# The first layer's late modulation on TensorE or on VectorE, in a two-layer hybrid trunk

## The chip, the cores and the metric

The kernel runs on one core of a Trainium2 chip. The metric is the device time of one execution, in microseconds (us), as the median of several. The engines are TensorE (PE, its weight loads PEld), VectorE (DVE), ScalarE (ACT), GpSimd (POOL) and SyncE (SP), which issues most transfers.

## The reference, cut to what matters

Two streams of tokens (1024 latent, 128 context) go through two layers and a last norm. Each layer takes six vectors per stream from a modulation: a product of one conditioning vector per stream (c and c_ctx) with a 1024 x 6144 weight.

```python
for l in range(DEPTH):                                  # 2 layers
    mod_ctx = silu(c_ctx)[None, :] @ w_mod[l] + b_mod[l]
    mod_lat = silu(c) @ w_mod[l] + b_mod[l]
    ...
def trunk_layer(x, mod, p, ...):
    sh1, sc1, g1, sh2, sc2, g2 = split(mod, 6)
    u = rmsnorm(x, norm1_g) * (1 + sc1) + sh1
    x = x + g1 * token_mixers(u)     # GLA | RG-LRU | Hyena | HGRN2
    u = rmsnorm(x, norm2_g) * (1 + sc2) + sh2
    x = x + g2 * ((silu(u @ w1) * (u @ w3)) @ w2)
```

The Hyena mixer needs filters that depend on weights alone: small networks, a decay, a normalisation and a cosine/sine transform, for both layers and for both sequence lengths ("s" for 1024 tokens, "p" for 128).

## The kernel before, in words

The whole kernel is one program without loops on the chip. Activations lie transposed, 128 channels by 1152 tokens, in large SBUF tiles of the pool `dp` (tag "d", 19 buffers of 128 x 2312 floats). Weights come in through SP into `wr` and are split into two parts by ACT and DVE (`wsplit`, L339 and L340); projections are three matmuls per 128 x 384 block.

The order of the work is made in two steps. Python generators say in which order it is written: a `main` generator is advanced turn by turn, and after each turn the queue `s.queue` of projections ("fill") is advanced by so many nanoseconds of TensorE work (`weave`, `WB = 1800`). The tile framework then lays out each engine's instruction stream ahead of the run; it may put an instruction or a transfer ahead of its written place when its operands and a free buffer are planned to be there, and each engine then runs its stream in order. SP's transfers are such a stream too.

The modulation comes in 12 chunks of 512 columns per layer (`c`), each in two loads (`i`) of 1024 KB into a "d" tile `wm` (L417). There are two ways to compute a chunk:

- `mods_pe` (L436): for each of 4 x 128 rows of a load and each of four 128-column pieces, one matmul with the conditioning columns `cT` (32 columns, two of them in use) as the stationary operand. The four pieces go to four groups of 32 partitions of one PSUM tile `ps` of tag "a". After each load there is a yield.
- `mods_dve` (L455): for each of 4 x 128 rows of a load and each of the two streams, one VectorE instruction multiplies 512 columns by a per-partition scalar and adds them to the accumulator `macc` (L466 for the first, L468 for the rest). There is a yield after each two, so four per load. After the second load eight small matmuls with `es` sum `macc` over the partitions.

Both end in `mod_out` (L423): ACT copies the PSUM tile to `mp`, one matmul with `sel8` puts it in place, DVE adds the bias; two yields.

Chunks 0 to 3 of the first layer (`NM[0] = 4`) are computed on TensorE at the start, beside the first filters and the loading of x; the first norm needs them. Chunks 4 to 11 come in `late()` in `main` (L1926), which takes turns with the remaining filters: `t1, s1` (taps and spectra of the second layer's "s" filter, 11 and 17 turns) and `tp0, sp0, tp1, sp1` (the "p" filters, 7 turns each), 56 turns in all. When `late` ends it queues `v_proj(0, 1, ...)`, a projection (9 blocks of 24 matmuls, 128 x 272). After the weave the first HGRN2 projections ("h0") are queued, and `layer` begins with the two RG-LRU units (`rg_core`: weight tile `rgw` at L1580, DVE convolutions L1002 and L1005 on `rgx`, matmuls, ACT and DVE chains on `rgri` and `rgab`). The second layer's modulation is computed with `mods_dve` in the first layer's feed-forward (`side`).

```python
def late():
    macc = s.d("macc")[:, :1024].rearrange("p (x n) -> p x n", x=2)
    yield from s.mods_dve(0, na, 12, macc, 1)
    s.fill_add([s.v_proj(0, 1, st.u, st.vh)], ("vh", 0))
s.weave(s.turns([ch(t1, s1, tp0, sp0, tp1, sp1), late()]), s.WB)
```

Of the kernel before, what the change touches and what calls it, by code (L numbers as in the profile page):

```python
# [277 lines left out]
class Trunk:  # L278
# [1550 lines left out]
    def main(s):  # L1829
# [5 lines left out]
        with tc.tile_pool(name="dp", bufs=19) as dp, tc.tile_pool(name="gp", bufs=1) as gp, \  # L1835
# [62 lines left out]
            for w, o in (("s", 0), ("p", 1152)):  # L1898
                n = HC[w]["Q"]
# [13 lines left out]
            na, nb = s.NM  # L1913
            for _ in s.turns([ch(t0, itertools.islice(s0, nb)), xi, s.mods_pe(0, 0, na, s.AH)]):
                pass
            x, xt, y = box
# [7 lines left out]
            s.x_out(0, xt)  # L1924

            def late():  # L1926
                macc = s.d("macc")[:, :1024].rearrange("p (x n) -> p x n", x=2)
                yield from s.mods_dve(0, na, 12, macc, 1)
                s.fill_add([s.v_proj(0, 1, st.u, st.vh)], ("vh", 0))
            s.weave(s.turns([ch(t1, s1, tp0, sp0, tp1, sp1), late()]), s.WB)  # L1930
            s.fill_add(s.hgrn_items(0, st.u, 0, st.hb[0]), ("h0", 0))
            for l in range(DEPTH):
# [15 lines left out]
```

## Time and profile before

| | |
|---|---|
| median of 3 runs | 3421.86 us (3419.73 to 3423.37) |
| profiled execution | 3423.5 us |
| its span, first to last instruction | 3421.7 us |
| PE busy | 3301.0 us (96%) |
| DVE busy | 1848.7 us (54%) |
| ACT busy | 1017.9 us (30%) |
| mean granted TensorE clock | 0.978 |

The granted clock is given as a share of 2.4 GHz: 1.00 is that level, 0.50 is 1.2 GHz, and a value between is a stretch that holds both. A busy time multiplied by it is the work as it would last at 2.4 GHz. Times in the trace count from the start of the span. A matmul of 32-bit floats appears as two records.

### The profile page before, as it was taken

Reading aid. Unit: us, or ns where it says so; the run is one execution under the profiler, and the core shown is the slowest. Engines: PE = TensorE matmul, PEld = TensorE weight load, DVE = VectorE, ACT = ScalarE, POOL = GpSimd, SP = SyncE. Lnnn points to the kernel's source line nnn. Section 1 sums busy time; section 2 is a strip of 40 time slices with the busy share of each in tenths; the row PEclk is TensorE's granted clock in tenths of the full one; section 3 lists DMA queues with packets and bytes.
Section 4 is the critical chain, followed back from the end, with each engine's and each line's share of the span. In section 5 each row is a group of like instructions: output and inputs, shape, how many; then the busy total and the mean of one; then the engine's idle time right before and its main releaser. Section 6 shows DMA issues by size and latency. Waiting matters only on the chain. (4 is left out here: it accounts for less than half of the span.)

```text
span 3421.7 us, 55255 instructions
## 1 busy us (share of the span) xinstructions
PE 3301.0 (96%) x23502; PEld 3036.4 (89%) x23502; DVE 1848.7 (54%) x3872; ACT 1017.9 (30%) x1831; POOL 28.4 (1%) x101
## 2 busy tenths in 40 slices
PE   7977999999999999999999999999999999999998
PEld 3525888889999999999999887889999999999998
DVE  6866677666664443444448578564845222222326
ACT  4424445332232111111124635533323111111122
POOL 0000000000000000000000000000000000000000
PEclk8977999999999999999999999999999999999999
DMA  7251110113312121222122010112411111111112
GB/s 273 96 181 59 33 38 22 47 58 139 115 56 84 58 87 56 87 74 84 56 84 85 29 56 16 33 64 100 154 37 45 36 48 38 43 41 47 44 44 74
DMA packets 72995, 241.10 MB, mean 70 GB/s; under 512 B 14319, under 2 KB 26469, under 8 KB 60972
## 3 DMA queue, kind: packets, MB, share of 16 engines
q1 hardware_dynamic: 70844, 223.22, 19.0%
q0 software_dynamic: 1904, 14.35, 1.2%
q8 instruction: 185, 3.03, 0.4%
q14 instruction: 62, 0.51, 0.0%
HBM read 207.99 MB, written 29.56 MB: 69 GB/s over the span
## 5 line engine op out<-in xcount | busy, mean ns | idle before, releaser
L296 PE MATMUL pm<-u,ws 128*128 128x384 f32 x9792 | 1807.8, 341 | 14.8 <-DVE DS L851 6.1
L296 PEld LDWEIGHTS pm<-u,ws 128*128 128x128 f32 x9792 | 1706.4, 188 | 47.9 <-issue 9.4
L296 PE MATMUL ps<-hid,ws 128*128 128x384 f32 x3168 | 557.5, 337 | 0.0
L296 PEld LDWEIGHTS ps<-hid,ws 128*128 128x128 f32 x3168 | 552.1, 188 | 0.6 <-DVE hid L1750 0.2
L339 ACT CAST ws<-wr 128x1024 fp32r<-128x1024 f32 (+3 forms) x234 | 220.3, 941 | 666.5 <-PE ps L296 401.9
L340 DVE TENSOR_TENSOR ws<-wr,ws 128x1024 fp32r<-128x1024 f32 (+3 forms) x234 | 254.5, 1088 | 221.3 <-ACT ws L339 220.3
L1748 DVE TENSOR_TENSOR sg<-sg,pm 128x384 f32<-128x384 f32 x132 | 72.9, 553 | 467.6 <-PE pm L296 467.6
L1492 DVE SCALAR_TENSOR_TENSOR x<-ps,mod,x 128x256 f32<-128x256 f32 (+1 forms) x320 | 158.1, 515 | 275.6 <-PE ps L296 274.5
L1749 ACT CAST hid<-sg 128x384 fp32r<-128x384 f32 x132 | 67.8, 513 | 476.3 <-DVE sg L1748 476.1
L296 PE MATMUL pm<-mh,ws 128*128 128x384 f32 x1152 | 204.1, 338 | 0.7 <-DVE x L1492 0.7
L296 PEld LDWEIGHTS pm<-mh,ws 128*128 128x128 f32 x1152 | 201.3, 188 | 1.6 <-DVE x L1492 1.4
L1742 ACT ACTIVATE sg<-pm 128x384 f32<-128x384 f32 x132 | 64.5, 489 | 226.7 <-PE pm L296 226.7
L296 PE MATMUL pm<-ws,u 128*128 128x272 f32 (+1 forms) x864 | 117.1, 292 | 3.7 <-ACT ws L339 2.2
L296 PEld LDWEIGHTS pm<-ws,u 128*128 128x128 f32 x864 | 109.7, 191 | 7.9 <-ACT ws L339 2.5
L468 DVE SCALAR_TENSOR_TENSOR acc<-wm,cT,acc 128x512 f32<-128x512 f32 x168 | 116.0, 744 | 0.0
L680 DVE COPY_PREDICATED DS<-masks,ps 128x192 f32<-128x192 uint8 x288 | 92.4, 367 | 33.9 <-PE ps L296 33.9
L1750 DVE TENSOR_TENSOR hid<-sg,hid 128x384 fp32r<-128x384 f32 x132 | 73.5, 557 | 58.4 <-ACT hid L1749 58.4
L296 PEld LDWEIGHTS ps<-QQ,kc 64*64 64x64 f32 x3456 | 68.5, 134 | 40.1 <-issue 27.8
L677 DVE TENSOR_TENSOR KK<-KK,TT 128x384 f32<-128x384 f32 x168 | 99.9, 597 | 7.1 <-PE ps L296 5.3
L681 DVE TENSOR_TENSOR QQ<-QQ,TT 128x384 f32<-128x384 f32 x168 | 100.1, 596 | 0.1
L296 PE MATMUL ps<-QQ,kc 64*64 64x64 f32 x3456 | 88.3, 231 | 7.7 <-DVE kc L658 4.7
L539 ACT ACTIVATE sq<-x 128x384 f32<-128x384 f32 x84 | 43.7, 523 | 142.1 <-DVE x L1492 109.0
(312 smaller groups left out, 2777.3 us busy)
## 6 DMA issues: line engine op xcount, KB each, us to landing
wm<-w_mod SPq DMA_DIRECT2D x48, 1024.0 KB, 6.3
wr<-w SPq DMA_DIRECT2D x96, 512.0 KB, 3.2
wr<-w_in SPq DMA_DIRECT2D x48, 512.0 KB, 3.6
dft<-dft_s POOLq DMA_DIRECT2D x12, 1152.0 KB, 7.5
wr<-w SPq DMA_DIRECT2D x32, 320.0 KB, 3.0
xscr<-x SPq DMA_DIRECT2D x8, 1152.0 KB, 10.7
x<-xscr SPq DMA_DIRECT2D x8, 1152.0 KB, 5.2
wr<-w_out SPq DMA_DIRECT2D x16, 512.0 KB, 3.8
```

Source lines behind the costliest of these rows:

```text
L296: return s.nc.tensor.matmul(out, lhsT, rhs, start=start, stop=stop)
L339: nc.scalar.copy(w[:, 0, :n], raw[:, :n])
L340: nc.vector.tensor_tensor(out=w[:, 1, :n], in0=raw[:, :n], in1=w[:, 0, :n].bitcast(F32), op=ALU.subtract)
L468: nc.vector.scalar_tensor_tensor(out=acc[:, x], in0=wk, scalar=cc, in1=acc[:, x], op0=ALU.mult, op1=ALU.add)
L677: nc.vector.tensor_tensor(out=ka, in0=ka, in1=cap(TT, o + GS + h, [[2 * h, n], [-(GS + h), 2], [0, h]]), op=ALU.mult)
L680: nc.vector.copy_predicated(Dt[:, g, j], s.masks[:, li].unsqueeze(1).to_broadcast([128, 3, 64]), ps[j])
L681: nc.vector.tensor_tensor(out=qa, in0=qa, in1=cap(TT, o + h, [[2 * h, n], [GS - h, 2], [0, h]]), op=ALU.mult)
L1492: nc.vector.scalar_tensor_tensor(out=x[k][:, a:b], in0=ps[:, a - g * GS:b - g * GS], scalar=gcol[:, k, st:st + 1], in1=x[k][:, a:b], op0=A ...
L1742: nc.scalar.activation(out=sg, in_=ps, func=AF.Silu)
L1748: nc.vector.tensor_tensor(out=sg, in0=sg, in1=pp[1], op=ALU.mult)
L1749: nc.scalar.copy(hi[:, 0, sl], sg)
L1750: nc.vector.tensor_tensor(out=hi[:, 1, sl], in0=sg, in1=hi[:, 0, sl].bitcast(F32), op=ALU.subtract)
```

## The change

`late()` computes chunks 4 to 11 of the first layer with `mods_pe` in place of `mods_dve`, with two loads ahead in place of one. The accumulator `macc` goes. The loads, their number and size, `mod_out` and the second layer's modulation stay as they are. `late()` has 4 yields for each chunk (two loads, two in `mod_out`) in place of 10, so 32 in place of 80.

```diff
             def late():
-                macc = s.d("macc")[:, :1024].rearrange("p (x n) -> p x n", x=2)
-                yield from s.mods_dve(0, na, 12, macc, 1)
+                yield from s.mods_pe(0, na, 12, 2)
                 s.fill_add([s.v_proj(0, 1, st.u, st.vh)], ("vh", 0))
```

The function that is called now:

```python
def mods_pe(s, l, c0, c1, ahead):
    todo = [(c, i) for c in range(c0, c1) for i in range(2)]
    q = collections.deque(s.mod_load(l, c, i) for c, i in todo[:ahead])
    for at, (c, i) in enumerate(todo):
        w = q.popleft()
        if i == 0:
            ps = s.p("a")[:, :128]
        for k in range(4):
            for j in range(4):
                s.mm(ps[32 * j:32 * j + 32], s.cT[:, 2 * (4 * i + k):2 * (4 * i + k) + 32],
                     w[:, 512 * k + 128 * j:512 * k + 128 * j + 128], start=(i == 0 and k == 0), stop=(i == 1 and k == 3))
        if at + ahead < len(todo):
            q.append(s.mod_load(l, *todo[at + ahead]))
        yield
        if i == 1:
            yield from s.mod_out(l, c, ps)
```

## Rows read from the trace of the kernel before

**Rows 1.** The page: busy us, share and count; PE's busy tenths in 40 slices.
```profile
PE 3301.0 (96%) x23502; PEld 3036.4 (89%) x23502; DVE 1848.7 (54%) x3872; ACT 1017.9 (30%) x1831; POOL 28.4 (1%) x101
PE   7977999999999999999999999999999999999998
```

**Rows 2.** Windows: stretch, length, PE PEld DVE ACT POOL busy (count), PEclk, DMA share, GB/s.
```profile
118.00:158.00 40.00, 36.26 (x180) 27.08 (x179) 33.67 (x58) 15.63 (x31) 0.00 (x0) 0.93 0.29 98
158.00:203.00 45.00, 42.58 (x123) 17.17 (x123) 30.97 (x48) 11.69 (x22) 0.00 (x0) 0.95 0.54 176
203.00:300.00 97.00, 57.61 (x185) 19.32 (x183) 80.21 (x137) 24.05 (x42) 0.00 (x0) 0.58 0.36 123
300.00:383.00 83.00, 77.06 (x440) 71.00 (x441) 41.55 (x53) 57.34 (x78) 0.00 (x0) 0.96 0.09 26
383.00:900.00 517.00, 504.52 (x5332) 449.06 (x5331) 357.25 (x882) 197.76 (x394) 12.74 (x40) 1.00 0.21 71
```

**Rows 3.** Windows of the tile macc alone: PE, PEld, DVE busy us (count).
```profile
118.00:158.00 40.00, 0.65 (x16) 0.38 (x16) 14.38 (x22) 0.93 0.29 98
158.00:203.00 45.00, 1.50 (x32) 0.69 (x32) 17.64 (x28) 0.95 0.54 176
203.00:300.00 97.00, 5.34 (x80) 2.31 (x80) 52.33 (x79) 0.58 0.36 123
```

**Rows 4.** Waits from 203 to 300 us: us in total, times, longest.
```profile
PE ps L296 <- DVE fX L1138: 12.8, 2, 7.1
PE ps L296 <- DVE fH L1181: 8.8, 2, 4.9
...
PE ps L296 <- DMA rgw<-rg_w: 5.8, 1, 5.8
```

**Rows 5.** Timeline of DVE inside the third filter's taps: start, us, instruction.
```profile
205.92 0.74 DVE L1131 SCALAR_TENSOR_TENSOR fH<-ps,fw,fwn 48x512 f32<-48x512 f32 x1
206.59 1.40 DVE L468 SCALAR_TENSOR_TENSOR macc<-wm,cT,macc 128x512 f32<-128x512 f32 x2
...
208.51 0.74 DVE L1131 SCALAR_TENSOR_TENSOR fH<-ps,fw,fwn 48x512 f32<-48x512 f32 x1
```

**Rows 6.** Tile wm: ns min/median/max, first and last start.
```profile
L468 DVE SCALAR_TENSOR_TENSOR macc<-wm,cT,macc x112: 621/744/754, 124.3 to 297.7; 128x512 f32<-128x512 f32 x112
L466 DVE TENSOR_SCALAR macc<-wm,cT x16: 466/481/487, 123.5 to 288.7; 128x512 f32<-128x512 f32 x16
```

**Rows 7.** Timeline of PE: start, us, matmuls and their count.
```profile
31.58 3.64 PE L296 MATMUL pa<-wm,cT 128*32 128x128 f32 x64
...
148.34 0.65 PE L296 MATMUL pa<-macc,es 128*32 128x128 f32 x16
...
255.60 1.08 PE L296 MATMUL pa<-macc,es 128*32 128x128 f32 x16
...
314.28 12.55 PE L296 MATMUL pm<-ws,u 128*128 128x272 f32 x96
...
330.35 10.12 PE L296 MATMUL pm<-u,ws 128*128 128x384 f32 x57
```

**Rows 8.** Timeline of SP's queue: start, us, transfer issued, count.
```profile
238.64 16.45 SPq L417 DMA_DIRECT2D wm<-w_mod  x6
...
275.96 0.39 SPq L1580 DMA_DIRECT2D rgw<-rg_w  x1
288.69 0.33 SPq L337 DMA_DIRECT2D wr<-w_vl  x1
```

**Rows 9.** Line 417 from 100 to 300 us: its loads, who waited, landing.
```profile
L417 SPq DMA_DIRECT2D wm<-w_mod x16: 327/383/1410, 116.9 to 274.5; - x16
...
  DVE macc L468: 1.7, 1
...
DMA to landing us min/median/max: 4.9/6.1/11.0
```

**Rows 10.** SP's own waits from 203 to 300 us.
```profile
SPq L1206 <- ACT fev L1204: 41.1, 8, 17.1
```

## The prediction

> **What bounds the kernel now.** I read the page first. TensorE is busy for 96% of the span, and its 40 slices are full except among the first few [rows 1]. So the kernel is a TensorE kernel with a poor beginning, and work that is put on TensorE is free only where TensorE stands idle or runs at its lower clock. Next come windows, cut where the character of the work changes [rows 2]. Busy time multiplied by the granted clock gives TensorE's work as it would last at 2.4 GHz: 36.26 x 0.93 = 33.7 us in 118 to 158, 42.58 x 0.95 = 40.5 in 158 to 203, 57.61 x 0.58 = 33.4 in 203 to 300, 77.06 x 0.96 = 74.0 in 300 to 383. As a share of the stretch: 0.84, 0.90, 0.34, 0.89. From 383 to 900 TensorE is busy for 504.5 of 517 us at full clock, and its slices stay full to the end [rows 1]. One stretch is bad: 203 to 300, where TensorE is half idle and, being fed so thinly, stands mostly on the 1.2 GHz level (0.58).
>
> In that stretch VectorE is busy for 80.2 of 97 us, and the tile `macc`, which is the late modulation alone, is 52.3 of these [rows 2, 3]. What TensorE waits for there is VectorE in front: the filters' sums and spectra (L1138, L1181: 12.8 and 8.8 us), then the transfer of `rgw` (5.8 us) [rows 4]. The timeline shows how: between two taps of a small filter stand two modulation instructions, 1.40 of the 2.59 us from tap to tap [rows 5]. The engine that delays TensorE is VectorE, and the modulation is two thirds of its load there. A second effect is seen on SP: loads of `wm` go out whenever a "d" buffer is free, six of them from 238.6 us, and the transfer of `rgw`, with which the RG-LRU units begin, goes out at 275.96, behind the last of them at 274.5; the last piece of weight for `v_proj` follows at 288.69 [rows 8, 9].
>
> **The change, part by part.**
>
> *VectorE's work goes.* 112 instructions of 744 ns and 16 of 481 ns [rows 6] are 91 us as single instructions; as time that they occupy it is 14.4 + 17.6 + 52.3 = 84.4 us [rows 3]. From 118 to 203 TensorE is nearly full anyway, so little of the first 32 us comes back there. From 203 to 300 VectorE keeps 80.2 - 52.3 = 27.9 us of work in 97.
>
> *TensorE's work comes.* A chunk is 64 records. The first four chunks ran this way already: 3.64 us for 64 at the lower clock. The `es` matmuls have the same shape, and 16 of them took 1.08 us at the lower clock and 0.65 at the full one, a ratio of 0.6 [rows 7]. So a chunk is 0.6 x 3.64 = 2.2 us, or 4 x 0.65 = 2.6 with a pause after each 16; eight chunks are 17 to 21 us at full clock and 29 at the lower one. I take 20, since the stretches that receive them run at 0.93 and 0.95. Away go the `es` matmuls, 0.65 x 0.93 + 1.50 x 0.95 + 5.34 x 0.58 = 5.1 us [rows 2, 3]. Net: 15 us more on the bound engine.
>
> *Order.* `late` takes 32 turns in place of 80, while the filters take 56 in both. Its chunks now stand beside the first 32 filter turns: seven chunks beside the 28 of `t1, s1`, the last beside `tp0`. Then `v_proj` is queued, 24 turns earlier than the filters' end, and 24 turns of 1800 ns call for more than its 9 blocks hold (216 records of 12.55 / 96 = 0.131 us, 28 us [rows 7]). So `v_proj`, whose last weights are asked for at 288.69 and whose end is at 330.4 us [rows 7, 8], is written beside the small filters, where TensorE is idle. The projections behind it ("h0") are all asked for before the first HGRN2 core in either program, so the order from there on should be the same, and the fill that stands in those waits is not used up.
>
> *Transfers and buffers.* The same 16 loads [rows 9], through the same queue. In the program two `wm` tiles stand in place of one and `macc`: the same number of buffers. They are done with by about 210 us instead of 298, which frees the buffers that `rgw` and the weights of `v_proj` wait for. I cost that at nothing by itself; it is what lets the next item happen. `mod_out` is unchanged, and its results for chunks 4 to 11 are used first at the output projection, far behind.
>
> *The sum, first way.* From 118 to 383 us TensorE holds 33.7 + 40.5 + 33.4 + 74.0 = 181.6 us of work at full clock. With 20 more and 5.1 less it is 196.5. If it were packed without a gap the 265 us would shrink by 68.5: that is the upper end. With the packing of the three good stretches (0.84, 0.90, 0.89, mean 0.88) it takes 223 us: **42 us saved**. With the worst of the three, 234: 31 saved.
>
> *The sum, second way.* In 203 to 300 the filters' own TensorE work is 57.6 - 5.3 = 52.3 us at the present clock, or about 30 at full clock, and VectorE has 27.9: so the filters need 30 to 52 us, and `v_proj` starts beside them, in place of 97. That saves 45 to 67. Seven chunks more (17.5 less 2.0 for `es`) lengthen 118 to 203 by 15.5 us less what VectorE no longer costs there; I estimate 10, from the 10.8 us by which its 85 us exceed the 74.2 us of work. Net 35 to 57, middle 46. I take 43 us between the two ways. The program from 383 on is TensorE-bound and shifts as a whole.
>
> The profiled execution took 3423.5 us, 1.8 of it outside its span and 1.6 over the median; 3423.5 - 43 is 3380.5, and on the median 3421.86 - 43 = **3379 us**.
>
> *A rule that speaks against it.* In the trace the lower clock is where TensorE is fed thinly: 0.58 from 203 to 300, against 0.93 and 0.95 where other matmuls stand between [rows 2]. The Trainium skill, in "TensorE: Matmul & The Clock Gate", section "Loop structure matters more than you think", calls a loop that waits for a transfer before every matmul the bad form, because the engine then runs cold. The 16 new batches are of that form if their loads come late. By that rule the 74.2 us of 118 to 203 would run at 1.2 GHz and last up to 74 us longer; by the rows, where filter matmuls stand between the batches, nothing is lost. What decides is the wait for the load, which is the first rival.
>
> **The rivals.**
>
> *TensorE waits for the loads: slower.* The engine runs its stream in order, so a batch whose load has not landed stops the filters and projections behind it. A load lands 6.1 us after its issue [rows 9], and a batch lasts about 1.2 us. With two in flight a load comes every 3.05 us, 49 us for 16, which fits into the 85 us of 118 to 203. But SP is in order too, and it waits for the filters' results before it stores them: 41.1 us in 203 to 300 [rows 10]; a load behind such a wait is late. At 4 us a batch the 16 cost 64 us against the 43: 3443 us. It decides from 43 / 16 = 2.7 us a batch on. Against it: where VectorE was the reader, its longest wait for a load was 1.7 us [rows 9].
>
> *Buffers, not VectorE, set the end of the stage: a small gain.* `v_proj` and `rgw` would still come only when the last small filter has given back its tiles. The last `wm` load and `rgw` go out at 274.5 and 276.0 [rows 8, 9], about when that happens. Then the stage ends at 263 to 275 plus 10 to 15 us for transfer and split, in place of 300: 10 to 27 us, so 3395 to 3412. For it: 19 buffers and the crowding of SP's queue. Against it: the modulation's tiles are among the holders.
>
> *Nothing comes back.* The RG-LRU units and the small filters are chains of ACT and VectorE; if they, and not VectorE's load, set the time to 383, the 15 us that TensorE gains as work fill its idle time: 3415 to 3428. Against it: VectorE busy for 83% of the stretch.
>
> **Chances and range.** Forecast (3362 to 3392, and to 3353 at the upper bound): 0.56. Small gain: 0.20. Nothing: 0.07. Slower: 0.17. Below 0.2%, 6.8 us, a measurement of this kernel can't tell a change; so faster 0.76, same 0.07, slower 0.17. The range leaves out the slower rival and a little below the forecast: 3352 to 3429.
>
> **What would show it.** In the changed profile: no `macc`; 512 records of `pa<-wm,cT` between about 118 and 215 us, at some 40 ns each; VectorE's share in 203 to 260 near half; `v_proj` (128 x 272) finished near 280 in place of 330; `rgw` issued before 230; the granted clock above 0.8 after 203; the first HGRN2 scores at about 340 in place of 383; from there the same distances to the end. The forecast is wrong if TensorE shows waits for `wm` of more than 2.7 us a batch, if `rgw` still goes out after 270, or if the stage ends early but the distance from the first scores to the end grows.

## The result, and the profile after

The changed kernel takes 3370.5 us (median of 4 runs, 3367.69 to 3371.02) against 3422.03 for the kernel before beside it (4 runs, 3419.73 to 3423.37). The ratio is 0.9848 with a 95% interval of 0.9831 to 0.9866: 51.5 us less, where 43 were forecast. The profiled execution is the fastest of the four, 3367.69 us with a span of 3365.9; against the span before of 3421.7, from an execution of 3423.5, that is 55.8 us.

The page of the changed kernel gives each engine's busy time, share and count, and then TensorE's busy tenths in 40 slices of 84 us:

```profile
PE 3288.5 (98%) x23886; PEld 3040.5 (90%) x23886; DVE 1767.6 (53%) x3744; ACT 1015.8 (30%) x1830; POOL 28.4 (1%) x101
...
PE   7999999999999999999999999999999999999998
```

VectorE has 81.1 us less [rows 1]; TensorE has 384 more matmul records and still 12.5 us less busy time, because more of its busy time lies at the 2.4 GHz level, where the same records are shorter (a chunk of 64 takes 2.16 us there and 3.64 at 1.2 GHz, as the last section shows). The dip of the third and fourth slices [rows 1] is gone. The windows (stretch, length, busy us and count of PE, PEld, DVE, ACT and POOL, granted clock, DMA share, GB/s) show where it went:

```profile
118.00:158.00 40.00, 40.00 (x359) 31.69 (x359) 20.75 (x33) 16.18 (x33) 0.16 (x3) 1.00 0.58 199
158.00:203.00 45.00, 42.44 (x338) 20.55 (x338) 13.78 (x27) 9.82 (x19) 0.00 (x0) 1.00 0.76 269
203.00:260.00 57.00, 57.00 (x352) 37.43 (x351) 26.70 (x53) 26.02 (x46) 0.00 (x0) 1.00 0.29 87
203.00:300.00 97.00, 97.00 (x520) 67.42 (x519) 40.18 (x71) 54.13 (x87) 0.00 (x0) 0.96 0.21 62
```

Against [rows 2], TensorE in 203 to 300 goes from 57.6 us busy at 0.58 to all 97 at 0.96, although the sixteen batches are now inside 118 to 213 us. VectorE's 80.2 us there become 40.2, and some of these 40 belong to later work that has moved in.

TensorE's timeline (start, us, engine, line, operation, tiles, shapes, count) shows the batches between filter matmuls, the end of `v_proj` (128 x 272), the last matmul of the small filters (`ps<-h,fex`) and the first HGRN2 scores:

```profile
174.34 1.08 PE L296 MATMUL pa<-wm,cT 128*32 128x128 f32 x32
175.36 5.42 PE L296 MATMUL ps<-fH,fM 128*128 128x512 f32 x12
...
211.78 1.08 PE L296 MATMUL pa<-wm,cT 128*32 128x128 f32 x32
...
251.27 3.26 PE L296 MATMUL pm<-ws,u 128*128 128x272 f32 x24
...
273.12 0.66 PE L296 MATMUL ps<-h,fex 34*48 34x512 f32 x1
...
322.47 1.61 PE L296 MATMUL ps<-DS,kd 64*64 64x64 f32 x48
```

A chunk is two batches of 32 records, 2 x 1.08 = 2.16 us. The same three marks in the trace before:

```profile
272.76 0.66 PE L296 MATMUL ps<-h,fex 34*48 34x512 f32 x1
...
327.15 3.36 PE L296 MATMUL pm<-ws,u 128*128 128x272 f32 x24
...
383.35 0.93 PE L296 MATMUL ps<-DS,kd 64*64 64x64 f32 x48
```

`v_proj` ends at 254.5 where it ended at 330.5, and the first scores come 60.9 us earlier. The small filters end where they did, at 273.8 against 273.4. On SP's queue the sixteen loads lie between 117.0 and 198.1 us, and the RG-LRU's weights go out at 242.2 where they went at 276.0 [rows 8]:

```profile
198.08 1.61 SPq L417 DMA_DIRECT2D wm<-w_mod  x1
212.28 0.35 SPq L337 DMA_DIRECT2D wr<-w_vl  x1
...
242.22 0.37 SPq L1580 DMA_DIRECT2D rgw<-rg_w  x1
```

TensorE's longest waits from 118 to 340 us (what it waited for, us in total, times, longest) have no filter sum on VectorE above 0.9 us any more, against 12.8 and 8.8 in [rows 4]:

```profile
PE ps L296 <- ACT DS L668: 2.5, 2, 1.3
PE pa L296 <- DMA wm<-w_mod: 1.6, 2, 1.3
PE pm L296 <- ACT KK L839: 1.2, 1, 1.2
PE ps L296 <- DVE fH L1174: 0.9, 1, 0.9
```

### The profile page after: what moved, and what is told of

Read it like the earlier page. It is cut to its first block, busy times and chain, and to the rows that moved or that the text cites. A ratio compares the mean times of both kernels' runs of the same rounds, so it can differ in the third digit from the quotient of the medians.

```text
span 3365.9 us, 55882 instructions
## 1 busy us (share of the span) xinstructions
PE 3288.5 (98%) x23886; PEld 3040.5 (90%) x23886; DVE 1767.6 (53%) x3744; ACT 1015.8 (30%) x1830; POOL 28.4 (1%) x101
## 5 line engine op out<-in xcount | busy, mean ns | idle before, releaser
L296 PEld LDWEIGHTS ps<-QQ,kc 64*64 64x64 f32 x3456 | 69.1, 134 | 42.2 <-issue 27.4
```

The lines of the kernel that those rows point to most:

```text
L296: return s.nc.tensor.matmul(out, lhsT, rhs, start=start, stop=stop)
```

## Experiments

Three things change together: the instructions move from VectorE to TensorE; the order changes, since `late` takes 32 turns for 80 and with it `v_proj` is queued earlier; and the sixteen weight tiles are held for a shorter time, in buffers that other loads want. The runs set them apart as far as they can. Edits are against the changed kernel unless it is said otherwise; "before" in the ratios is always the kernel before on the same chip. The interval of a ratio is 0.001 to 0.002 either way, so a difference between two of these kernels is known to 7 or 8 us. Rows of waits are from 118 to 340 us unless it is said otherwise.

**1. VectorE's load alone.** TensorE does the modulation as in the changed kernel, and VectorE executes its 128 former instructions as well, into an accumulator that nobody reads.

```diff
+            if acc is not None:
+                for k in range(4):
+                    for x in range(2):
+                        wk, cc = w[:, 512 * k:512 * k + 512], s.cT[...]
...
+                        s.nc.vector.scalar_tensor_tensor(out=acc[:, x], in0=wk, scalar=cc, in1=acc[:, x], ...)
...
-                yield from s.mods_pe(0, na, 12, 2)
+                yield from s.mods_pe(0, na, 12, 2, macc)
```

> The changed kernel, with VectorE's 128 modulation instructions put back beside the matmuls: they write an accumulator that nobody reads. TensorE's work and the written order are those of the changed kernel. If the gain of 51.5 us came from VectorE's relief, most of it goes: 3395 to 3425 us, with TensorE waiting for the filters' VectorE steps (L1138, L1174, L1181) again and the clock below 0.8 somewhere between 203 and 300. If the gain came from the order (v_proj written 24 turns earlier, beside the small filters), it stays: 3370 to 3382.

Measured: 3412.73 us (8 runs, 3407.32 to 3415.12), ratio 0.9973 [0.9963, 0.9984]. That is 42.2 us over the changed kernel: four fifths of the gain are lost with TensorE's instructions and the turns of `late` unaltered. Windows, waits and SP's queue of this kernel:

```profile
158.00:203.00 45.00, 29.22 (x174) 14.14 (x175) 41.23 (x67) 5.66 (x11) 0.00 (x0) 0.70 0.35 117
203.00:300.00 97.00, 89.41 (x541) 53.16 (x540) 61.99 (x108) 29.16 (x54) 0.00 (x0) 0.86 0.42 138
```

```profile
PE pa L296 <- DMA wm<-w_mod: 11.0, 4, 5.1
PE ps L296 <- DVE h L1199: 4.1, 1, 4.1
PE ps L296 <- DVE fH L1182: 3.8, 1, 3.8
```

```profile
285.37 0.38 SPq L1588 DMA_DIRECT2D rgw<-rg_w  x1
```

The longest wait is not for VectorE but for a load. A tile is now given back only when VectorE has read it, so the load behind it is late. VectorE itself stands idle for 10.4 us before modulation instructions whose load has not landed. This run doesn't say whether VectorE's time or its hold on the tiles costs the 42 us; run 7 asks that.

**2. The order alone, on VectorE.** The kernel before, with `late` pausing after every fourth step: 32 turns.

```diff
-                yield
+                if k % per == per - 1:
+                    yield
```

> The kernel before, modulation on VectorE, but with one yield per load in place of four, so that late() takes 32 turns and v_proj is written where the changed kernel has it. If VectorE's load was the limit: 3400 to 3422, within 20 us of before. If the order was: 3360 to 3380, that is as fast as the changed kernel or faster, since TensorE also has 12 us less to do.

Measured: 3411.57 us (10 runs, 3409.67 to 3416.14), ratio 0.9975 [0.9965, 0.9984]: 9.6 us of the 51.5 median difference. The windows and waits of this kernel:

```profile
158.00:203.00 45.00, 22.99 (x75) 10.59 (x76) 38.50 (x64) 7.42 (x14) 0.00 (x0) 0.65 0.30 105
203.00:300.00 97.00, 87.16 (x396) 49.39 (x394) 66.53 (x115) 30.38 (x55) 0.00 (x0) 0.89 0.47 149
```

```profile
PE pa L296 <- DVE macc L468: 25.5, 5, 10.8
```

The same wait from 158 to 203 alone:

```profile
PE pa L296 <- DVE macc L468: 14.1, 2, 10.8
```

`v_proj` does fill 203 to 300, which reads 0.89 where it read 0.58 [rows 2]. But the `es` matmuls, which add up VectorE's result, now stand earlier in TensorE's stream, VectorE is not done, and TensorE waits 25.5 us for it from 118 to 340, 14.1 of them in 158 to 203. With VectorE as the worker the early order moves the hole forward.

**3. The old order with TensorE as the worker.** 48 empty turns before `v_proj` is queued.

```diff
+                for _ in range(48):
+                    yield
```

> The changed kernel with 48 empty turns before v_proj is queued, so that late() lasts 80 turns as before. If VectorE's relief is what counts: 3370 to 3385, since the matmuls of v_proj can still be laid ahead where TensorE is planned idle. If the order is: 3395 to 3420.

Measured: 3390.01 us (3387.36 to 3391.28), ratio 0.9908 [0.9893, 0.9923]: 31.1 less than before, 19.5 more than the changed kernel. It falls between the two expectations: neither the order nor the engine has it alone. The window of 203 to 300:

```profile
203.00:300.00 97.00, 84.39 (x375) 46.10 (x374) 43.11 (x72) 47.99 (x75) 0.00 (x0) 0.75 0.15 42
```

VectorE is free here and TensorE is still thinly fed (375 records for 520), waiting 8.1 us for spectra of the small filters, with nothing else queued to stand between. Runs 2 and 3 make a table with the two kernels: on VectorE 3422.0 (80 turns) and 3411.6 (32), on TensorE 3390.0 and 3370.5. The move between the engines is worth 32 to 41 us, the order 10 to 20. Each seems to be worth more once the other is done, but the 10 us between the two readings are little more than the intervals leave open.

**4. What TensorE's new work costs.** The late chunks are left out: their values are a constant, nothing is loaded or multiplied for them, and the 32 turns stay.

```diff
-                yield from s.mods_pe(0, na, 12, 2)
+                s.nc.vector.memset(s.mod[0][:, 4 * na:], 0.1)
+                for _ in range(32):
+                    yield
```

> The changed kernel without chunks 4 to 11 of the first layer's modulation: their values are set to a constant, their 16 loads and 512 matmul records are left out. It measures what they still cost. If TensorE is the limit there, the 8 chunks (64 records in 2.1 us each) cost their whole length, 17 us: 3350 to 3357. If they still lie in idle time of TensorE: 3366 to 3371.

Measured: 3354.09 us (3352.75 to 3356.63), ratio 0.9805 [0.979, 0.982]: 16.4 us below the changed kernel, whose batches are 17.1 us busy. So the total changes by about TensorE's time for them, as on an engine that is the bound. The loads, the tiles and the small matmuls of `mod_out` are gone as well, and this run can't tell their part from TensorE's; the first scores come only 10.2 us earlier (312.25), and where the rest is saved was not followed.

**5. Half and half.** Chunks 4 to 7 on TensorE, 8 to 11 on VectorE, 32 turns in all.

```diff
-                yield from s.mods_pe(0, na, 12, 2)
+                yield from s.mods_pe(0, na, 8, 2)
+                macc = ...
+                yield from s.mods_dve(0, 8, 12, macc, 1, 4)
```

> Chunks 4 to 7 on TensorE, 8 to 11 on VectorE (one yield per load, so 32 turns and v_proj written as in the changed kernel). VectorE gets half its old load back, 42 us, and TensorE loses four chunks: 4 x (2.16 - 0.65) = 6 us. In the changed kernel VectorE is busy for 13.8 of 45 us in 158 to 203 and for 40.2 of 97 in 203 to 300, so 42 us more would fit by share. If only VectorE's share of the stretch counts: 3362 to 3368, faster than the changed kernel. If VectorE's place in order counts, that is, if filter steps must queue behind modulation steps: 3376 to 3395.

Measured: 3380.49 us (3379.01 to 3385.28), ratio 0.9885 [0.9869, 0.9902]: 10.0 over the changed kernel. Half the VectorE work costs a quarter of what the whole cost in run 1, though TensorE has only 5.6 us less of its own (four chunks of 2.16 us, less 3.06 for the `es` matmuls that come back); TensorE's wait for `macc` is one of 3.8 us.

**6. The second layer's modulation on TensorE as well.**

```diff
-        side = s.mods_dve(l + 1, 0, 12, macc, 1) if l < DEPTH - 1 else iter(())
+        side = s.mods_pe(l + 1, 0, 12, 2) if l < DEPTH - 1 else iter(())
```

> The changed kernel with the second layer's modulation on TensorE as well, in the first layer's feed-forward, where TensorE is full and VectorE half idle. Twelve chunks of 64 records at 2.16 us less 12 x 0.65 us for the es matmuls: 18 us more on TensorE. If TensorE's added work counts in full where it is full: 3386 to 3392. If VectorE's modulation delays that stage too, the two cancel: 3366 to 3375.

Measured: 3387.75 us (3387.43 to 3388.6), ratio 0.9905 [0.989, 0.9919]: 17.3 over the changed kernel. The first scores come where they do in the changed kernel (322.0 us). In the feed-forward of the changed kernel TensorE is busy for 779.7 of the 780 us from 960 to 1740, at a clock of 1.00 and with no wait for VectorE, so there the same move only costs.

**7. VectorE's time without the hold on the tiles.** As run 1, but the 128 instructions read the accumulator, not the weights, so a weight tile goes back as soon as TensorE has read it. One "d" tile, `macc`, is still held.

```diff
-                        wk, cc = w[:, 512 * k:512 * k + 512], s.cT[...]
+                        wk, cc = acc[:, 1 - x], s.cT[...]
```

> As e1_dve_load, the changed kernel with VectorE's 128 instructions beside the matmuls, but they read the accumulator and not the loaded weights, so they hold no weight buffer: the wm tiles come free when TensorE is done with them. One tile is still held for the accumulator. If VectorE's time is what e1_dve_load lost: 3400 to 3415. If it was the weight buffers kept by slow readers (the transfer of rgw went out at 285 us there): 3375 to 3390.

Measured: 3388.35 us (3387.57 to 3391.17), ratio 0.9907 [0.9893, 0.9922]: 24.4 below run 1, 17.9 over the changed kernel. VectorE spends no less on it (91.8 us on `macc` in 118 to 300, against 82.1 in run 1). The windows and SP's queue:

```profile
158.00:203.00 45.00, 40.64 (x297) 20.24 (x298) 41.90 (x69) 8.35 (x17) 0.00 (x0) 0.85 0.61 207
203.00:300.00 97.00, 89.34 (x492) 55.72 (x491) 72.77 (x126) 35.08 (x63) 0.00 (x0) 0.89 0.31 95
```

```profile
264.51 0.38 SPq L1588 DMA_DIRECT2D rgw<-rg_w  x1
```

So the theory that VectorE's time alone is the cost fell: with a VectorE that is as busy, TensorE in 158 to 203 has 297 records for run 1's 174, and `rgw` goes out 21 us earlier. More than half of the 42 us needs VectorE as a *reader* of the tiles. That is two things at once: a reader holds the tile, and it waits for the load (the 10.4 us of run 1, which are gone here); this run does not part them. In runs 1 and 7 nobody waits for the accumulator either, so what the `es` matmuls wait for in run 2 is in neither price.

**8. One buffer less.** One of the 19 "d" buffers is held idle from the start of `late` to the end of the filters.

```diff
+                held.extend(s.d("held")[:, :8] for _ in range(1))
...
+            for h in held:
+                s.nc.vector.tensor_copy(s.tmp("hq", 8), h)
```

> The changed kernel with one of the 19 large buffers taken out of use from the start of the late modulation to the end of the filters. VectorE's load is that of the changed kernel. If buffers are what the stage lacks: 3385 to 3405. If VectorE's time is: 3368 to 3376.

Measured: 3379.25 us (3371.43 to 3382.66), ratio 0.9876 [0.986, 0.9892]: 8.8 over the changed kernel, between the two expectations. Its four runs all lie above those of the changed kernel (3371.43 to 3382.66 against 3367.69 to 3371.02), but the two intervals overlap, so that the 8.8 are known only to about 8. The `rgw` load is 12.7 us later than after, and 203 to 300 reads:

```profile
203.00:300.00 97.00, 93.18 (x482) 58.94 (x482) 35.48 (x67) 42.31 (x72) 0.00 (x0) 0.89 0.25 77
```

```profile
254.93 0.37 SPq L1580 DMA_DIRECT2D rgw<-rg_w  x1
```

A buffer has a price in this stage, of uncertain size. In run 7 the held `macc` would account for some 9 of the 17.9 us, and about as much would be left for VectorE's time; that split adds two runs, was not measured by one, and is no firmer than the 8.8.

**9 to 11. Fewer tiles for the late weights.** The sixteen loads go through fixed tiles, taken once: two in run 9, one in run 10 (both from the changed kernel), one in run 11 (from the kernel before). In run 10 two loads are still issued ahead, so a batch multiplies the columns that the load behind it has brought; the number of instructions and bytes is the same.

```diff
-        w = s.d("wm")[:, :2048]
+        if l == 0 and c >= s.NM[0]:
+            s.wmt = getattr(s, "wmt", None) or [s.d("wm") for _ in range(2)]
+            w = s.wmt[(2 * c + i) % 2][:, :2048]
+        else:
+            w = s.d("wm")[:, :2048]
```

> The changed kernel with its 16 late loads going into two large tiles in turn, held from the first load to the last use, in place of as many as happen to be free. If buffers taken by early loads still hold back rgw and the weights of v_proj: rgw is issued before 235 and the time is 3362 to 3369. If the loads need the extra buffers to hide their landing: 3374 to 3390, with TensorE waiting for wm.

> As e9_pe_two_tiles with a single tile, so that a load is issued only when the matmuls of the one before are done. TensorE then waits for each load unless other work stands between: a load lands 6 us after its issue, the filter work between two batches is about 2.6 us, so up to 16 x 3.4 = 54 us if nothing else is laid between: 3371 to 3425. With other work laid between, as the plan can: 3366 to 3385. It sizes the rival of the prediction in which TensorE waits for the loads.

> The kernel before, modulation on VectorE and 80 turns, with its 16 late loads through a single tile. VectorE's work is the same, but the loads can no longer take every buffer that is free. If the buffers held by loads that wait for VectorE delayed v_proj and rgw: 3390 to 3410. If VectorE's time did: 3415 to 3435, as the loads now come one by one.

Run 9: 3373.17 us (3367.49 to 3374.82), ratio 0.9853 [0.9836, 0.9869], the changed kernel's within the interval; neither branch of its expectation, which had a gain or a loss. `rgw` goes at 243.9 and TensorE waits 1.8 us for `wm`. Holding the changed kernel's loads to two tiles neither gains nor costs anything that shows.

Run 10: 3386.92 us (3386.44 to 3387.42), ratio 0.9896 [0.9881, 0.9911], 16.4 over the changed kernel. The window of 158 to 203 and TensorE's wait of this kernel:

```profile
158.00:203.00 45.00, 40.83 (x274) 20.28 (x270) 13.53 (x26) 8.50 (x17) 0.00 (x0) 0.82 0.55 183
```

```profile
PE pa L296 <- DMA wm<-w_mod: 8.9, 5, 3.3
```

The same wait from 158 to 203 alone:

```profile
PE pa L296 <- DMA wm<-w_mod: 4.9, 3, 2.9
```

This is the rival of late loads, made on purpose: five waits, three of them in 158 to 203, where the clock reads 0.82 in place of 1.00.

Run 11: 3406.17 us (3402.37 to 3409.02), ratio 0.9952 [0.9937, 0.9966], 16.0 below the kernel before, whose only change is that the late weights take one tile in place of as many as are free. The window (all work, then the tile `macc` alone), the waits and SP's queue of this kernel:

```profile
203.00:300.00 97.00, 75.05 (x274) 37.25 (x273) 69.59 (x122) 39.21 (x65) 0.00 (x0) 0.67 0.35 116
203.00:300.00 97.00, 3.01 (x48) 1.50 (x48) 36.16 (x56) 0.67 0.35 116
```

```profile
PE ps L296 <- DVE fH L1185: 12.6, 2, 9.8
PE ps L296 <- DVE fX L1142: 8.5, 3, 6.7
```

```profile
240.42 0.42 SPq L1584 DMA_DIRECT2D rgw<-rg_w  x1
```

`rgw` goes as early as in the changed kernel (240.4 and 242.2), and TensorE still waits for VectorE's filter sums as in [rows 4]. So 16 us come back without the change. They are not the buffers' part alone: with one tile the late loads come later, 24 of VectorE's 128 instructions run after 300 us, and `macc` takes 36.2 us of the bad stretch where it took 52.3 [rows 3]. What a shorter hold on the tiles gains and what this relief of VectorE in the bad stretch gains, the run does not part.

**12. Both repairs on VectorE.** Runs 2 and 11 together, on the kernel before: 32 turns and one tile.

> e2_dve_32turns and e11_dve_one_tile together: modulation on VectorE, 32 turns, one tile for the late loads. It has all that the change brings in order and in buffers, and VectorE's load of before. If order (9.6 us) and buffers (16 us) add up: 3392 to 3400, and what is left to the changed kernel, some 25 us, is VectorE's time alone. If the two are one and the same effect (the place where v_proj and rgw can begin): 3402 to 3410. If VectorE's time is worth little: 3370 to 3385.

Measured: 3441.67 us (3440.42 to 3443.24), ratio 1.0065 [1.0048, 1.0081]: 21 us *slower* than before, where each edit alone was faster; all that I expected fell. The waits of TensorE, of VectorE, and SP's queue:

```profile
PE pa L296 <- DVE macc L472: 47.9, 6, 10.8
...
DVE macc L472 <- DMA wm<-w_mod: 26.7, 6, 10.0
```

```profile
313.50 0.37 SPq L1585 DMA_DIRECT2D rgw<-rg_w  x1
```

The early order puts the `es` matmuls early into TensorE's stream; with one tile, VectorE's instructions come load by load; TensorE stands behind both. It is a third chain, made by the two repairs, so this run does not measure VectorE's part.

## Why the prediction was right, step by step

*What bounds the kernel* held in part: 203 to 300 was the hole, and it is closed. That VectorE alone digs it was too simple. The small filters, from their first tap to their last matmul, take 72.5 us before (200.9 to 273.4) and 65.0 after (208.8 to 273.8); in run 3, where VectorE is free and `v_proj` comes late, they take 67.6. So VectorE's relief shortens them by 5 to 8 us only, and their end does not move. What moved is the other work. From 203 to that end TensorE was busy for 45.1 of 70.4 us at a clock of 0.53, and now for all 70.8 at 0.98, with `v_proj` and the first HGRN2 projections between the filter matmuls; from there to 300, where TensorE was busy for 12.5 of 26.6 us while `rgw` and the last weights of `v_proj` came in, it is now busy throughout. Runs 1, 7, 8 and 11 show that both VectorE's work and its hold on the tiles keep that other work out: of run 1's 42 us, 24 go when VectorE no longer reads the tiles. How the two compare in size is not shown.

*VectorE's work goes*: yes; no `macc` is left before the first scores, and VectorE has 26.7 of 57 us in 203 to 260, a share of 0.47 where "near half" stood.

*TensorE's work comes*: 512 records are 17.1 us, the lower end of 17 to 21; 20 were taken. Run 4, where they, their loads and `mod_out` are gone, is 16.4 us faster, about what work on the bound engine would cost.

*Order* held in direction. `v_proj` ended at 254.5, not near 280, and beside the small filters, as was said. Run 3 puts the old order's price at 19.5 us on TensorE; run 2 shows that the same order gives 9.6 while VectorE is the worker. I had no number for the order by itself.

*Transfers and buffers*, "I cost that at nothing by itself", is the step that failed. One buffer costs 8.8 us (run 8, known to about 8), VectorE's reading of the tiles costs 24 (runs 1 and 7), and loads that take one tile are worth 16.0 on the kernel before, VectorE's later work included (run 11). Its landmark failed with it: `rgw` went out at 242.2, not before 230. As a landmark it says when buffers come free, not what is gained: it went out at 240.4 and 239.3 in runs 11 and 3 as well, whose times are 35.7 and 19.5 us above the changed kernel's. The sum survived because its first way works with the whole stage, so the buffers' part was inside without a name.

The Trainium skill, in "Perfetto Trace Analysis", section "Optimization Strategy", says that gaps which repeat on the engine that ought to be full can mean that there are too few buffers for the next tile. The rows of before named VectorE and a transfer as what TensorE waited for, never a buffer, so the cause that the skill gives could not be read from them. What runs 8 and 11 show of buffers is a transfer that goes out at another time: `rgw` at 254.9 with one buffer less than the changed kernel (242.2), and at 240.4 with one tile for the late weights (276.0 before).

*The sum, first way.* The mis-sized term is the packing. 0.88 was the mean of the three good stretches; after, it is (40.00 x 1.00 + 42.44 x 1.00 + 97.00 x 0.96) / 182 = 0.965. With that and 17.1 in place of 20, the work of 193.6 us takes 200.6, 64 less than 265; the first scores came 60.9 earlier. Counted in the trace, the 204.5 us from 118 to the first scores hold 40.00 + 42.44 + 97.00 x 0.96 + 21.10 = 196.7 us of work (the last 22.5 us at a clock of 1.00), a packing of 0.96, so the 196.5 us of the prediction were right and 0.88 was not. In two of the three stretches that gave 0.88 VectorE still had its load; the third, 300 to 383, had none of it and read 0.89. Why the stage packs better than all three is not shown.

*The sum, second way.* It let the small filters end 30 to 52 us after 203 in place of 97. Their last matmul ended 70.4 us after 203 before and 70.8 after, so no time came from there, and that its net of 35 to 57 us holds the 51.5 measured is in part luck. `v_proj` does stand beside the filters, but in their waits, not because they end sooner.

*The program from 383 on shifts as a whole*: nearly. 60.9 us at the first scores are 55.8 at the end of the span, so the distance from there to the end grew, which the prediction had named as a sign against it; it grew by 5 us. These go at once, in the first RG-LRU and HGRN2 units, which now begin with less fill behind them. The 20.5 us from the first scores on, after and then before:

```profile
322.50:343.00 20.50, 16.64 (x181) 15.38 (x181) 17.93 (x22) 15.76 (x23) 0.00 (x0) 0.83 0.02 4
383.35:403.85 20.50, 20.50 (x258) 18.66 (x258) 14.04 (x29) 6.54 (x15) 0.00 (x0) 1.00 0.19 56
```

TensorE now has 3.9 idle us there at a clock of 0.83, while VectorE and ACT are busy; before it had none, at 1.00. That the fill was used up is argued from these rows, not tested. That the medians differ by 51.5 and not by 55.8 is the spread of runs: the profiled execution is the fastest of its four, and the one before was 1.6 us above its median.

*The rule that speaks against it.* The clock is 1.00 in 118 to 203 and the waits for `wm` are 1.6 us in 2, so the case of the page ("TensorE: Matmul & The Clock Gate", "Loop structure matters more than you think", in the Trainium skill) did not arise: filter matmuls stand between the batches. Run 10 makes it arise in part, with 4.9 us of waits and a clock of 0.82 in 158 to 203, and the trace agrees with the rule.

*The rivals.* TensorE waiting for the loads fell: two waits of 1.6 us in all, against 2.7 us for every batch. "Nothing comes back" fell. "Buffers, not VectorE" fell in its time (3370.5 against 3395 to 3412) and in its order: `v_proj` was done at 254.5, before the last small filter at 273.8. But its mechanism is real and was worth a place among the terms.

**What stays open.** How the 51.5 us divide between VectorE's time, its hold on the tiles, and the order can't be given as three numbers: run 12 shows that they do not add. No run is faster than the changed kernel with the same computation; run 9 equals it.

## What to carry to other kernels

When an engine in front of the bound one is relieved, ask also what it was *holding*: a slow last reader keeps load buffers, and the cost appears elsewhere as a transfer that goes out late. Ask, too, whether the chain that you relieve ends sooner, or only lets other work in beside it. The packing of the stretches around is no bound for a stage (0.88 taken, 0.96 measured). Try order, engine and buffers one at a time, and together, before adding their worths. The same move is worth its price only where the bound engine has idle or low-clock time: 51.5 us gained in the first layer, 17.3 lost in the second.

## What the runs showed that was not expected

- Two edits that gain 9.6 and 16.0 us alone lose 21 together (runs 2, 11 and 12).
- The small filters end at 273.4 us before and 273.8 after, though VectorE lost 52 us of work between 203 and 300; the gain is in what TensorE does beside them.
- One idle buffer of 19 costs 8.8 us (run 8, known to about 8), with TensorE still busy for 93.2 of 97 us in the bad stretch: of the work that this stretch loses (93.18 x 0.89 for 97.00 x 0.96, 10.2 us) the clock is about two thirds.
- A chunk on TensorE is 2.16 us at the full clock and 3.64 at the lower one: 0.59, where the clocks stand as 0.50. The granted clock at the chunk of [rows 7] reads 1.00, though it takes 3.64 us; the third chunk before, at 49.74, takes as long where it reads 0.50. Batches between filter matmuls stand without a pause, but for the two waits for `wm`.
